# Row sums of a 16384 x 1024 matrix: VectorE takes the sixth whole block row by row as sums of halves

## The chip, the core and the metric

The kernel runs on one core of a Trainium2 chip. A time is the device time of one execution in microseconds (us). The time before is the median of three runs, 161.60 us, with runs from 161.56 to 161.78. A profile is one execution that the hardware profiler recorded; its times count from the first instruction of the recorded execution, and it is without the small stretch outside the program's first and last instruction.

## The reference

The input `x` is 32 x 512 x 1024 in fp32, 64 MiB. The output is the sum over the last axis, 32 x 512 numbers in fp32:

```python
def reference(x):
    return np.sum(x, axis=-1).astype(np.float32)
```

Every input number is read once and added once. The kernel is therefore a stream from device memory (HBM) to on-chip memory (SBUF), with sums that have to keep up with it.

## The kernel before

The 16384 rows are seen as eight blocks of 128 partitions x 16 rows x 1024 numbers. A block is 8 MiB, 64 KB in each partition. Block 7 is split: its first 7 rows are loaded first of all, and its other 9 rows last of all, in pieces of 6 rows, 2 rows, 536 numbers and 488 numbers of a row. Between them come the whole blocks 0 to 6 in order. So the stream is: 7 rows, blocks 0, 1, 2, 3, 4, 5, 6, then 6 rows, 2 rows and the two pieces of the last row.

`rows` (L177) loads a block, or a part of one, by one DMA from SyncE's queue (L180) and has it summed. There are two ways of summing on VectorE:

- `vec` (L140): one TENSOR_REDUCE over all the rows of the block, with one sum for each row.
- `halves` (L153): for each row one instruction that adds the first half of the row (512 numbers) to the second half, writes the 512 sums over the first half in place, and accumulates the sum of all. A second short instruction, DVE_READ_ACCUMULATOR2_ANT, writes the accumulated sum out. `rows` uses it where `pairs=True`.

ScalarE takes `n_act` of the rows (L166, an ACTIVATE with an accumulator and its readout; what it writes beside that goes unread to PSUM).

Blocks 0 to 5 and the first 7 rows are summed by `vec`, wholly on VectorE. Block 6 has 9 rows by `halves` and 7 rows on ScalarE. Of the last rows, the load of 6 has 4 rows by `halves` and 2 on ScalarE, the load of 2 has one of each, and the last row is summed in two pieces by two calls of `halves`, the second of which takes the first's sum in. "The sixth whole block" is block 5.

The order of the work on each engine is the order in which the kernel writes it (a manual schedule). The input tiles go round three buffers, which this text calls A, B and C: the first rows use A, then blocks 0 B, 1 C, 2 A, 3 B, 4 C, 5 A, 6 B, and the remaining rows of block 7 C. A load into a buffer waits until the sums of the buffer's earlier contents are done. The load of block 3 therefore waits for the sums of block 0, that of block 4 for block 1, that of block 5 for block 2, that of block 6 for block 3, and the last loads for block 4. No load follows into the buffers of blocks 5 and 6. SyncE issues loads strictly in order, so one that waits holds up those behind it. The load of block 1 is also held until the first rows are summed.

The sums of blocks 0 to 6 (56 KB) are stored by one DMA from ScalarE's queue, held until the load of two rows has landed; the sums of block 7 (8 KB) by one DMA of SyncE at the very end (L191 through L227).

## Time and profile before

| quantity | value | from |
|---|---|---|
| time, median of three runs | 161.60 us | the times |
| span of the profiled execution (its own time, first to last instruction) | 160.3 us | the page |
| difference of the two | 1.3 us | subtraction |
| VectorE busy | 120.6 us, 75% | the page |
| ScalarE busy | 11.9 us, 7% | the page |
| load queue (q1) | 67.12 MB, 97.7% of 16 DMA engines | the page |
| VectorE's sum of one whole block by one instruction | 17.22 us | groups by form |
| VectorE's sum of one row by halves | 0.689 us and a readout of 0.084 us | groups by form |

The page does not give a time of the profiled execution other than its span. A row of the groups names the line, the engine, the operation and the tile that it writes and reads, then the count, the busy time, the mean time of one in ns, and the idle time of the engine just before, with what ended it. The chain that ended last runs in time from the start to the end and names at each step what the next one waited for. In it the load steps overlap the sums before them, since a load is issued long before it is waited for.

The loads land, by the starts of the sums that wait for them, at 11.0 (7 rows), 30.3, 49.7, 69.1, 88.5, 108.0, 127.5 (block 5), 147.1 (block 6), 154.3 (6 rows), 156.8 (2 rows) and 158.1 us (the last piece).

### The profile page before, as it was taken

Reading aid. Unit: us, or ns where it says so; the run is one execution under the profiler, and the core shown is the slowest. Engines: PE = TensorE matmul, PEld = TensorE weight load, DVE = VectorE, ACT = ScalarE, POOL = GpSimd, SP = SyncE. Lnnn points to the kernel's source line nnn. Section 1 sums busy time; section 2 is a strip of 40 time slices with the busy share of each in tenths; the row PEclk is TensorE's granted clock in tenths of the full one; section 3 lists DMA queues with packets and bytes.
Section 4 is the critical chain, followed back from the end, with each engine's and each line's share of the span. In section 5 each row is a group of like instructions: output and inputs, shape, how many; then the busy total and the mean of one; then the engine's idle time right before and its main releaser. Section 6 shows DMA issues by size and latency. Waiting matters only on the chain.

```text
span 160.3 us, 132 instructions
## 1 busy us (share of the span) xinstructions
DVE 120.6 (75%) x40; ACT 11.9 (7%) x21; POOL 0.2 (0%) x4
## 2 busy tenths in 40 slices
DVE  0029600499986999679995999949999499994955
ACT  3000000000000000000000000000000000003993
POOL 0000000000000000000000000000000000000000
DMA  8999999899799699699699699796996996996994
GB/s 300 386 491 523 392 392 523 376 409 523 327 458 523 294 491 523 262 523 523 262 523 523 262 523 441 343 523 278 507 523 262 523 523 262 523 523 264 423 384 123
DMA packets 2784, 67.18 MB, mean 419 GB/s; under 512 B 1248, under 2 KB 1376, under 8 KB 1504
## 3 DMA queue, kind: packets, MB, share of 16 engines
q1 hardware_dynamic: 1872, 67.12, 97.7%
q10 hardware_dynamic: 912, 0.06, 0.4%
HBM read 67.11 MB, written 0.07 MB: 419 GB/s over the span
## 4 chain that ended last, share of the span: by engine, by line
DMA 71%; DVE 27%; SPq 1%; issue 0%; DVEq 0%
DMA t<-in_x_dram 71%; DVE sums L141 26%; SPq L180 0%; SPq L222 0%; DVE t L155 0%; DVEq L253 0%
## 5 line engine op out<-in xcount | busy, mean ns | idle before, releaser
L141 DVE TENSOR_REDUCE sums<-t 128x16 f32<-128x16384 f32 (+1 forms) x7 | 110.9, 15848 | 33.8 <-DMA t<-in_x_dram 33.8
L168 ACT ACTIVATE unread<-t 128x1024 f32<-128x1024 f32 x10 | 10.1, 1012 | 145.3 <-DMA t<-in_x_dram 145.3
L155 DVE CUSTOM_DVE_ANT_0 t<-t 128x512 f32<-128x512 f32 (+2 forms) x16 | 9.6, 656 | 4.1 <-DMA t<-in_x_dram 4.0
L168 ACT ACTIVATION_READ_ACCUMULATOR unread<-t 128x1 f32 x10 | 1.9, 187 | 0.0
L168 ACT ACT_TABLE_LOAD x1 | 1.3, 1283 | 0.8 <-PEq L242 0.8
L155 DVE DVE_READ_ACCUMULATOR2_ANT sums<- 128x1 f32 x15 | 1.3, 84 | 0.0
L242 POOL MEMSET const-bfloat16-1.0<- 128x1 bf16 x1 | 0.1, 101 | 0.0
L242 POOL MEMSET const-uint8-127<- 128x1 uint8 x1 | 0.1, 101 | 0.0
L242 POOL MEMSET const-float32-0.0<- 128x1 f32 x1 | 0.1, 98 | 0.2 <-issue 0.2
L242 POOL MEMSET const-float32-1.0<- 128x1 f32 x1 | 0.1, 98 | 0.0
L155 DVE DVE_READ_ACCUMULATOR2_ANT t<- 128x1 f32 x1 | 0.1, 83 | 0.0
L220 DVE MEMSET t<- 128x1 f32 x1 | 0.1, 59 | 0.0
## 6 DMA issues: line engine op xcount, KB each, us to landing
t<-in_x_dram SPq DMA_DIRECT2D x1, 3584.0 KB, 11.0
t<-in_x_dram SPq DMA_DIRECT2D x1, 3072.0 KB, 29.0
t<-in_x_dram SPq DMA_DIRECT2D x1, 1024.0 KB, 31.1
t<-in_x_dram SPq DMA_DIRECT2D x1, 268.0 KB, 31.4
t<-in_x_dram SPq DMA_DIRECT2D x1, 244.0 KB, 31.4
t<-in_x_dram SPq DMA_DIRECT2D x7, 41.1
out_dram<-sums ACTq DMA_DIRECT2D x1, 56.0 KB, 2.1
out_dram<-sums SPq DMA_DIRECT2D x1, 8.0 KB, 1.4
```

What stands on the lines that cost most here:

```text
L141: return nc.vector.tensor_reduce(out=dst, in_=src, axis=mybir.AxisListType.X, op=mybir.AluOpType.add)
L155: return nc.vector.tensor_tensor_reduce(out=src[:, :n], in0=src[:, :n], in1=src[:, n:], scale=1.0, scalar=0.0, op0=mybir.AluOpType.add, op ...
L168: nc.scalar.activation(out=unread[:, :n], in_=src, func=mybir.ActivationFunctionType.Copy, accum_out=dst,)
L220: nc.vector.memset(whole[:, width + 1 :], 0.0)
L242: nc = _bacc.Bacc("TRN2", target_bir_lowering=False, num_devices=1)
```

## The change

Block 5 is summed by `halves`, row by row, in place of one TENSOR_REDUCE over its 16 rows. Blocks 0 to 4 stay with `vec`, and block 6 stays as it was.

```diff
         for g in range(last):
             t = inpool.tile([P, BIG * dim + 4], fp32)
             if g < last - 1:
-                load = rows(t, 0, BIG, g * BIG, 0)
+                load = rows(t, 0, BIG, g * BIG, 0, pairs=g == last - 2)
             else:
                 rows(t, 0, BIG, g * BIG, 7, pairs=True)
```

On VectorE one TENSOR_REDUCE goes, and 16 sums of halves with 16 readouts come in its place, at the same place in the order; one wait on VectorE's own semaphore is added ahead of them, for the last reader of the buffer before (the sums of block 2), because `halves` writes into the tile. VectorE's whole program grows from 51 to 83 instructions, waits and barriers among them. The instructions of SyncE, ScalarE, GpSimd and TensorE are the same as before, in the same order.

## The prediction

> **What bounds the kernel now.** I began with the chain of work that ended last, because only work on it can move the end. Its second half, in the order of time (start, length, what), and after it three rows of the timeline (the same columns, with the idle time before in brackets):

> ```profile
> 66.94 41.09 DMA t<-in_x_dram
> 108.03 0.02 issue
> 108.05 17.23 DVE sums L141
> 125.28 0.02 issue
> 125.30 0.33 SPq L180
> ...
> 126.65 31.45 DMA t<-in_x_dram
> 158.09 0.04 issue
> 158.13 0.42 DVE t L155
> ```

> ```profile
> 108.05 17.22 DVE L141 TENSOR_REDUCE sums<-t 128x16 f32<-128x16384 f32 x1 [2.29 <-DMA t<-in_x_dram]
> ...
> 127.53 17.22 DVE L141 TENSOR_REDUCE sums<-t 128x16 f32<-128x16384 f32 x1 [2.27 <-DMA t<-in_x_dram]
> ...
> 147.06 0.69 DVE L155 CUSTOM_DVE_ANT_0 t<-t 128x512 f32<-128x512 f32 x1 [2.31 <-DMA t<-in_x_dram]
> ```

> The last sum of VectorE that the chain passes through is the one from 108.05 to 125.28, block 4: its end frees buffer C, SyncE issues the last four loads (125.30 to 127.1), and from then on the chain is the load stream up to 158.09, then 0.42 us of VectorE and the small store. Block 5's sum, the one that changes, runs from 127.53 and is not on it. Even the sum of block 4 is only on the chain by name: what it released was queued behind block 6's load, which landed at 147.06, more than 20 us later. So next I looked at the stream by stages, each from one landing to the next (columns: the stretch, its length, busy time of VectorE, ScalarE, GpSimd, then clock, DMA share, GB/s):

> ```profile
> 11.02:30.34 19.32, 7.62 (x1) 0.00 (x0) 0.00 (x0) 1.00 1.00 434
> 30.34:49.69 19.35, 17.22 (x2) 0.00 (x0) 0.00 (x0) 1.00 1.00 434
> 108.05:127.53 19.48, 17.22 (x1) 0.00 (x0) 0.00 (x0) 1.00 1.00 431
> 127.53:147.06 19.53, 17.22 (x1) 0.00 (x1) 0.00 (x0) 1.00 0.91 396
> 147.06:154.34 7.28, 5.60 (x18) 7.28 (x14) 0.00 (x0) 1.00 0.99 426
> 154.34:156.84 2.50, 2.50 (x8) 2.19 (x5) 0.00 (x0) 1.00 0.97 400
> ```

> A block takes 19.3 to 19.5 us to land and 17.22 us to sum. VectorE waits about 2.3 us in each stage for data. The DMA engines are full throughout. The kernel is bound by the load stream, with a short tail behind its last piece. (The GB/s of a stretch depends on where the records put its large packets, so the 396 of the fourth row is not read as a slow stage; the landing at 147.06, 19.53 us after the one before, is what counts.) Last, the groups by form, for durations:

> ```profile
> L141 DVE TENSOR_REDUCE sums<-t 128x16 f32<-128x16384 f32 x6 | 103.3, 17220 | 22.8 <-DMA t<-in_x_dram 22.8
> L155 DVE CUSTOM_DVE_ANT_0 t<-t 128x512 f32<-128x512 f32 x14 | 8.8, 689 | 4.0 <-DMA t<-in_x_dram 4.0
> L155 DVE DVE_READ_ACCUMULATOR2_ANT sums<- 128x1 f32 x15 | 1.3, 84 | 0.0
> ```

> **The change part by part.**

> *Removed:* one TENSOR_REDUCE of 17.22 us, from 127.53 to 144.75. *Added:* 16 sums of halves and 16 readouts. They overlap: in block 6 the nine row sums start at 147.06, 147.68, 148.29 and so on to 151.96 in the timeline, (151.96 - 147.06) / 8 = 0.6125 us apart. Sixteen rows take 15 x 0.6125 + 0.69 = 9.88 us, so block 5 should be summed at about 127.53 + 9.88 = 137.41, which is 144.75 - 137.41 = 7.3 us sooner.

> *Who waits for that end?* On VectorE, the sums of block 6, and they wait for a landing at 147.06: VectorE was idle 2.31 us before them and will be idle about 9.65. On SyncE, nothing: the last loads were issued from 125.30 to 127.1 on the end of block 4, before block 5's sum starts, and buffer A gets no later load. On ScalarE's queue, the store of the first seven blocks needs the sums, but it is also held until two rows land and was issued at 156.93, 12 us after block 5 was done. So the 7.3 us become idle time, worth 0 us. The cover is the landing of block 6. It would be gone only if block 5's sum ended after 147.06, that is if it took over 19.53 us, twice what I work out.

> *The added wait* on VectorE's own semaphore asks for the sums of block 2, done at 86.27 (69.05 + 17.22), 41 us before. The waits of this kind took 0.02 us each in the trace. It lies ahead of block 5's sums and behind block 4's, where VectorE waits 2.27 us for data anyway. Behind it stand only block 5's own sums. Cost 0 us, and 0.02 us if it came after the landing, which block 6's idle time would swallow.

> *A longer idle time ahead of block 6* is the one new state of VectorE. After 11.70 us of idle time it took up block 0 at 30.34 with the usual delay of 0.02 us and the usual 17.22 us, so I take 0.

> *What the new instructions do to the stream* is the only term that can move the end, since the stream of block 6 runs beside them. TENSOR_REDUCE reads SBUF and writes almost nothing; the halves read the same data and write half of it back (512 of 1024 numbers a row), in a shorter time. The trace of before has this beside loads only from 147.06 on. The 6-row load landed in 7.28 us with 5.60 us of VectorE beside it, almost all of it halves: 1.213 us a row. A row under TENSOR_REDUCE took 19.32 / 16 = 1.208 to 19.53 / 16 = 1.221 us. For six rows that is between 6 x (1.2133 - 1.2075) = +0.035 us and 6 x (1.2133 - 1.2206) = -0.04 us, by 5.6 us of halves; for 9.9 us of halves +0.06 to -0.08 us. A farther row gives the upper end: the 2-row load took 2.50 us, all of it under VectorE's halves, against 2 x 1.2075 = 2.415, so 0.085 us by 2.50 us, or +0.34 us by 9.9 us. [...] I take 0, from the 6-row load, which is the nearest in size, and keep +0.34 as the upper end.

> *Less of TENSOR_REDUCE beside the stream* could also be a gain. The stage with only 7.62 us of it took 19.32 us, stages with 17.22 us took 19.35 to 19.53: at most 0.21 us by 9.6 us, or 0.16 us for the 7.3 us that go. The stage of 19.35 with full VectorE work says that most of this is something else (0.03 by 9.6 us, or 0.02). I take 0 and keep -0.16 as the lower end.

> *Code.* 32 more instructions must be fetched. Inside the span the page's DMA queues are q1 and q10 alone, loads and stores; in the 12 us before the span there is another:

> ```profile
> DMA packets 13, 0.05 MB, mean 4 GB/s; under 512 B 7, under 2 KB 7, under 8 KB 7
> ## 3 DMA queue, kind: packets, MB, share of 16 engines
> q14 instruction: 13, 0.05, 1.4%
> ```

> Seven of the 13 packets are small, so six carry 0.05 MB, some 8 KB each, in 1.4% x 16 x 12 = 2.7 us of one engine: at most 0.45 us each. If 32 more instructions need one more such packet inside the span, one of the 16 DMA engines is late by up to 0.45 us, and by nothing at the end if it is not the last one. I take 0, since 83 instructions follow a program of 51 that needed none, and keep +0.45.

> *Sum:* 0 us on a span of 160.3 us; with the 1.3 us around it, the median of 161.6 stands as the forecast.

> [...]

> **The rivals.** What this kernel's measurement can tell from no change is about 0.2%, 0.32 us.

> 1. *Slower by a code fetch.* For it: the instruction queue exists, and VectorE's program is 63% longer. Against: none of its packets lies in the span before, with five engines' programs. Price: up to +0.45 us, 162.05, if the packet falls on a DMA engine that lands last. It passes the 0.32 us only in that case. If instead VectorE itself had to wait for code, it has 9.6 us of room up to 147.06 and 1.68 us more from 152.66 to 154.34.
> 2. *Slower by writes.* The in-place writes of halves hold up the stream's writes. For it: the 2-row load. Against: the 6-row load. Price: up to +0.34 us, 161.94, and it decides only at that upper end.
> 3. *Faster by less reading.* The shorter work of VectorE lets block 6 land sooner. For it: 19.32 against 19.53. Against: 19.35 with full work. Price -0.16 us, 161.44, which is still within 0.2%; it shows as faster only together with a favourable draw of runs.
> [...]

> **How the numbers follow.** The forecast (nothing moves, rival 4 included) has 0.72; the code fetch 0.11, the writes 0.10, the reading 0.07. Within 0.2% falls nearly all of the first (0.68, leaving 0.02 on each side for the two programs' runs not being alike), and of the others 0.03, 0.02 and 0.02: 0.75. Slower: 0.02 + 0.08 + 0.07 = 0.17, with 0.01 of the writes going the other way; faster: 0.02 + 0.05 + 0.01 = 0.08. The range goes down to rival 3 less the spread of runs, 161.44 - 0.12, about 161.3, and up to rivals 1 and 2, 162.0.

> **What would show it.** In the changed profile: 16 sums of halves from about 127.5 to 137.4, VectorE idle about 9.6 us before 147.1; landings at 127.5, 147.1, 154.3, 156.8 and 158.1 as before; q1 and q10 alone among the queues. Rival 1 would add an instruction queue to the span, rival 2 a landing of block 6 later than 19.53 us after block 5, rival 3 an earlier one. The prediction is wrong if block 6 lands more than 0.3 us off, or if VectorE begins block 6 later than its landing.

## The result and the profile after

The changed kernel takes 162.35 us (median, runs from 162.27 to 162.56) against 161.58 for the kernel before: ratio 1.0046, 95% interval 1.0033 to 1.0058. Run again beside the experiments it took 162.32, ratio 1.0035 (1.0023 to 1.0047). It is slower by 0.63 to 0.77 us by the medians. The forecast of no change was wrong, and the range ended at 162.0.

The profiled execution took 162.27 us with a span of 160.5. First the timeline of VectorE after (start, length, what, idle time before and what ended it; rows left out are marked by dots):

```profile
107.95 17.22 DVE L141 TENSOR_REDUCE sums<-t 128x16 f32<-128x16384 f32 x1 [2.13 <-DMA t<-in_x_dram]
...
127.30 0.69 DVE L155 CUSTOM_DVE_ANT_0 t<-t 128x512 f32<-128x512 f32 x1 [2.13 <-DMA t<-in_x_dram]
...
146.66 0.69 DVE L155 CUSTOM_DVE_ANT_0 t<-t 128x512 f32<-128x512 f32 x1 [9.47 <-DMA t<-in_x_dram]
...
154.60 0.69 DVE L155 CUSTOM_DVE_ANT_0 t<-t 128x512 f32<-128x512 f32 x1 [2.34 <-DMA t<-in_x_dram]
```

VectorE did what was forecast: block 5 from 127.30 to 137.19, then 9.47 us of idle time until block 6 lands. Nothing waited for it. The loss is further on. The stages after, each from one landing to the next (columns as in the prediction):

```profile
107.95:127.30 19.35, 17.22 (x1) 0.00 (x0) 0.00 (x0) 1.00 1.00 434
127.30:146.66 19.36, 9.89 (x33) 0.00 (x1) 0.00 (x0) 1.00 0.94 408
146.66:154.60 7.94, 5.60 (x19) 7.39 (x15) 0.00 (x0) 1.00 0.97 413
154.60:157.05 2.45, 2.45 (x7) 2.20 (x5) 0.00 (x0) 1.00 0.88 352
```

Block 6, whose load runs beside the new instructions, took 19.36 us, as the block before it did with its TENSOR_REDUCE. The load of six rows took 7.94 us, where it took 7.28 before: 0.66 us lost, in a stage in which VectorE and ScalarE do exactly what they did before. The queues of the page after have a line that the page before does not have:

```profile
q1 hardware_dynamic: 1872, 67.12, 97.3%
q10 hardware_dynamic: 912, 0.06, 0.4%
q14 instruction: 1, 0.01, 0.0%
```

and the half microsecond from 153.0 to 153.5 has it:

```profile
q1 hardware_dynamic: 34, 0.19, 98.6%
q14 instruction: 1, 0.01, 4.1%
```

One packet of code, 8 KB, lies at the time of the six-row load; 4.1% of 16 engines over 0.5 us is 0.33 us of one DMA engine. The chain ends as before, only later:

```profile
126.52 31.76 DMA t<-in_x_dram
158.27 0.02 issue
158.30 0.42 DVE t L155
```

The two profiled spans, 160.3 and 160.5, differ by only 0.2 us. Every later run has its span: 31 runs of the kernel before on one chip had a median of 159.8 (159.6 to 160.4), with 1.78 us around it, which is the time less the span. The execution that the prediction was read from was half a microsecond longer than most: its stages from 69 us on took 19.48 to 19.53 us, while those above took 19.35 and 19.36 (the execution above has two such longer stages early, of 19.49 and 19.47 us). Against 159.8, the changed kernel's median span of 160.5 has the whole loss, and the 1.78 us around it are the same.

### The profile page after: what moved, and what is told of

Read it like the earlier page. It is cut to its first block, busy times and chain, and to the rows that moved or that the text cites. A ratio compares the mean times of both kernels' runs of the same rounds, so it can differ in the third digit from the quotient of the medians.

```text
span 160.5 us, 164 instructions
## 1 busy us (share of the span) xinstructions
DVE 113.2 (71%) x71; ACT 12.0 (7%) x21; POOL 0.2 (0%) x4
## 4 chain that ended last, share of the span: by engine, by line
DMA 71%; DVE 26%; SPq 1%; issue 0%; DVEq 0%
DMA t<-in_x_dram 71%; DVE sums L141 26%; SPq L180 0%; SPq L222 0%; DVE t L155 0%; DVEq L253 0%
## 5 line engine op out<-in xcount | busy, mean ns | idle before, releaser
L141 DVE TENSOR_REDUCE sums<-t 128x16 f32<-128x16384 f32 (+1 forms) x6 | 93.7, 15620 | 31.4 <-DMA t<-in_x_dram 31.4
L155 DVE CUSTOM_DVE_ANT_0 t<-t 128x512 f32<-128x512 f32 (+2 forms) x32 | 19.4, 670 | 14.1 <-DMA t<-in_x_dram 14.1
L155 DVE DVE_READ_ACCUMULATOR2_ANT sums<- 128x1 f32 x31 | 2.5, 81 | 0.0
L155 DVE DVE_READ_ACCUMULATOR2_ANT t<- 128x1 f32 x1 | 0.1, 83 | 0.0
```

What stands on the lines that cost most here:

```text
L141: return nc.vector.tensor_reduce(out=dst, in_=src, axis=mybir.AxisListType.X, op=mybir.AluOpType.add)
L155: return nc.vector.tensor_tensor_reduce(out=src[:, :n], in0=src[:, :n], in1=src[:, n:], scale=1.0, scalar=0.0, op0=mybir.AluOpType.add, op ...
```

## The experiments

The code theory: VectorE's longer program makes it fetch one more block of code inside the span, and that packet puts back the DMA engine that it falls on, so that every load behind it lands late. A border, below, is in this theory the place in VectorE's program behind which another block of code is needed. The write theory: the in-place writes of the halves hold up the stream.

**The instructions without the writes.** The kernel before with 32 memsets, each of which writes one number that nobody reads:

```diff
         first = sums_of[-1]
+        spare = stpool.tile([P, 32], fp32)
+        for k in range(32):
+            nc.vector.memset(spare[:, k : k + 1], 0.0)
```

> The kernel before, with 32 one-number memsets on VectorE ahead of block 0's sum, where VectorE is idle for 11.7 us (18.65 to 30.34); block 5 is summed by one TENSOR_REDUCE as before. VectorE's program has 83 instructions, as many as the changed kernel. Code theory (one more code packet inside the span holds up one DMA engine): the queue q14 shows one packet inside the span at about 153 us, the 6-row load lands about 7.9 us after block 6 in place of 7.28, and the time is 0.3% to 0.6% above before (162.1 to 162.5). Write theory (the in-place writes of halves hold up the stream): no row by halves more than before, so no difference, 161.6.

Measured: 162.24 us, ratio 1.0036 (1.0024 to 1.0049), span 160.5. The loss is there in full, with block 5 summed as before. Its timeline, and its instruction queue between 153.0 and 153.5:

```profile
127.18 17.22 DVE L141 TENSOR_REDUCE sums<-t 128x16 f32<-128x16384 f32 x1 [2.13 <-DMA t<-in_x_dram]
146.62 0.69 DVE L155 CUSTOM_DVE_ANT_0 t<-t 128x512 f32<-128x512 f32 x1 [2.22 <-DMA t<-in_x_dram]
154.54 0.69 DVE L155 CUSTOM_DVE_ANT_0 t<-t 128x512 f32<-128x512 f32 x1 [2.33 <-DMA t<-in_x_dram]
```

```profile
q14 instruction: 1, 0.01, 3.9%
```

Six rows take 154.54 - 146.62 = 7.92 us, and the packet is where it was in the changed kernel.

**The writes without the instructions.** Block 5 by two instructions, the heart of the edit:

```diff
+                nc.vector.tensor_tensor(
+                    out=block[:, :, :half],
+                    in0=block[:, :, :half],
+                    in1=block[:, :, half:],
+                    op=mybir.AluOpType.add,
+                )
+                sums_of.append(vec(sums[:, j : j + nv], block[:, :, :half]))
```

> Block 5 by two instructions: one TENSOR_TENSOR that adds the halves of all 16 rows and writes them in place (the same bytes read and written in place as in the changed kernel), then one TENSOR_REDUCE over 16 x 512. The number of VectorE's instructions is as before, 51. VectorE should be at it for about 8.6 + 8.6 = 17.2 us. Code theory: no packet inside the span, 161.6. Write theory: the same loss as the changed kernel, 162.3, and block 6 lands late.

Measured: 161.64 us against 161.59, ratio 1.0007 (0.9998 to 1.0017), span 159.85 by the median, no packet of code in the profiled span. In the timeline the add with its in-place writes runs beside block 6's load:

```profile
127.73 8.69 DVE L183 TENSOR_TENSOR t<-t 128x8192 f32<-128x8192 f32 x1 [2.22 <-DMA t<-in_x_dram]
136.45 8.69 DVE L141 TENSOR_REDUCE sums<-t 128x16 f32<-128x8192 f32 x1
146.99 0.69 DVE L155 CUSTOM_DVE_ANT_0 t<-t 128x512 f32<-128x512 f32 x1 [1.85 <-DMA t<-in_x_dram]
```

Block 6 lands 19.26 us after block 5. The write theory falls: the same bytes written, in 8.69 us in place of 9.89, cost nothing that this measurement can tell.

**The packet at another place.** The changed kernel with 64 memsets, as in the first run, ahead of block 0's sum (147 instructions).

> The changed kernel, with 64 memsets in the same place. Code theory: VectorE crosses the border in its code early, at about 20 us, so the packet on q14 lies there and not at 153 us; the engine that is held up is late by the same amount for all that follows, so the time is again 0.3% to 0.6% above before, unless the engines' differences later swallow it. A second packet would show that the border recurs after fewer than 85 instructions. Write theory: as the changed kernel, 162.3, and the place of the packet is of no account.

Measured: 162.25 us, ratio 1.0035 (1.0023 to 1.0047), one packet, at 24.8 us. VectorE's timeline:

```profile
18.55 1.09 DVE L203 MEMSET spare<- 128x1 f32 x60
20.02 0.15 DVE L203 MEMSET spare<- 128x1 f32 x4 [0.38 <-issue]
31.01 17.22 DVE L141 TENSOR_REDUCE sums<-t 128x16 f32<-128x16384 f32 x1 [10.84 <-DMA t<-in_x_dram]
50.35 17.22 DVE L141 TENSOR_REDUCE sums<-t 128x16 f32<-128x16384 f32 x1 [2.12 <-DMA t<-in_x_dram]
```

Block 0 now lands at 31.0 in place of 30.3, and all that follows stays late by that. The same 0.65 us are paid at the other end of the stream. After 60 memsets VectorE stops for 0.38 us. With three instructions ahead of the block of the kernel and one sum, that is after its 64th instruction.

**How far the borders lie apart.** The kernel before with 192 memsets at that place.

> The kernel before with 192 memsets on VectorE in the idle time ahead of block 0's sum (some 15 ns each by the run with 32, 3 us of 11.7): 243 instructions. If code comes in packets of 8 KB that hold 128 instructions, VectorE crosses two borders, about its 62nd and its 190th instruction, both between 18 and 22 us: two packets on q14 inside the span. If each holds up one DMA engine by 0.65 us, the time is 0.65 above before when they fall on two engines (162.25) and 1.3 above when they fall on the same one (162.9). If packets are larger than 8 KB apart in the code, one packet alone and 162.25.

Measured: 163.35 us, ratio 1.0097 (1.0084 to 1.0109). VectorE's timeline:

```profile
18.62 1.09 DVE L203 MEMSET spare<- 128x1 f32 x60
20.10 3.63 DVE L203 MEMSET spare<- 128x1 f32 x128 [0.38 <-issue]
26.50 0.15 DVE L203 MEMSET spare<- 128x1 f32 x4 [2.78 <-issue]
31.94 17.22 DVE L141 TENSOR_REDUCE sums<-t 128x16 f32<-128x16384 f32 x1 [5.28 <-DMA t<-in_x_dram]
```

The borders stand after the 64th and the 192nd instruction, 128 apart, and there is a packet for each, at 24.7 and 30.4 us. Two packets cost 1.66 us, and block 0 lands at 31.9, with one of its 16 completions 1.55 us behind the next. If each of the 16 completions stands for one of the 16 DMA engines, two engines held up once each would leave two completions late; by that reading both packets fell on the same engine. The 0.38 us at the first border can't have been a wait for its packet, which came 4.6 us later, when VectorE was past the border; for which instructions the packet was, no run shows. At the second border VectorE stopped for 2.78 us and went on 1.5 us after the end of the first packet. That it had come there before its code would fit, but the profile doesn't show what it waited for.

**A border crossed when the loads are through.** The same edit with 16 memsets, 67 instructions.

> The kernel before with 16 such memsets: 67 instructions, so that VectorE reaches its 62nd at the very end of its work, when the last loads have landed or are about to. Code theory: the packet comes too late to hold up a load; what it costs depends on whether VectorE has to wait for it. If the fetch is ahead of need, 161.6 to 161.8; if the end of the program waits for it as in the run with three rows by halves, 0.4 us outside the last instruction or at the end of the span, 162.0; 162.25 would say that the place does not matter and the theory of the held-up engine is wrong.

Measured: 161.81 us against 161.69, ratio 1.0014 (1.0003 to 1.0024); the one packet lies at 160.0, behind the last load and just behind the span. The 6-row load lands 7.29 us after block 6. VectorE's 65th instruction begins 0.54 us after the 64th; in each of the other runs, the same two instructions of the program's end lie 0.11 apart. So the border is where the runs above put it, and of a stop of 0.42 us there at most 0.2 shows in the time. 16 more instructions cost about 0.1 us by the medians and 0.2 by the ratio, 32 cost 0.65.

**A border just behind the program.** Of block 5 only three rows by halves, 57 instructions (an excerpt; the call for block 5 sets `few`):

```diff
+            if few:
+                sums_of.append(vec(sums[:, j + 3 : j + nv], block[:, 3:nv, :]))
+                for q in range(3):
+                    sums_of.append(halves(sums[:, j + q : j + q + 1], block[:, q, :]))
```

> The kernel before, but of block 5 three rows are summed by halves and 13 by TENSOR_REDUCE: 57 instructions on VectorE in place of 51. Code theory: no packet inside the span (in the changed kernel it came when VectorE had come to about its 62nd instruction), and the time of before, 161.6 within 0.1. Write theory: 3/16 of the changed kernel's loss, about 0.15 us, 161.7.

Measured: 162.07 us, ratio 1.0025 (1.0012 to 1.0037), which neither theory had. The span is as before, 159.9 by the median, without a packet; the stretch around it is 2.18 us, where the kernel before has 1.78. So I tried the number of instructions alone, six memsets in place of the three rows:

> The kernel before with 6 memsets ahead of block 0's sum: 57 instructions on VectorE, as in the run with three rows by halves, and nothing else of that run. If the 0.4 us outside the span in that run come of the number of instructions, they come again: span 159.8, stretch around it 2.17 in place of 1.78, 162.0. If they came of the three rows by halves, 161.6.

Measured: 162.03 us, ratio 1.0025 (1.0013 to 1.0037), span 159.8, 2.20 us around it. It goes with the number. That the 0.4 us are a stop at the border, in code that runs behind the kernel's last instruction, fits the border after the 64th and the 0.42 us of the run with 16 memsets, but the profile shows nothing there, so it stays an argument.

**Whose code.** GpSimd with 100 memsets, VectorE as before (the line inside the loop):

```diff
+            nc.gpsimd.memset(spare[:, k : k + 1], 0.0)
```

> The kernel before with 100 one-number memsets on GpSimd, which has no other work, from the start on; VectorE's program is as before, 51 instructions. Code theory: any engine's code packet holds up the stream, so q14 shows one packet in the first 15 us or so and the time is 162.25. If only VectorE's code matters (it stands ahead of the sums), 161.6.

Measured: 161.84 us against 161.69, ratio 1.0004 (0.9995 to 1.0014), with an 8 KB packet at 6.1 us. Either the early time or the engine made it cheap. Two pairs of runs tell these apart. VectorE early, in the kernel before and in the changed one:

```diff
+        for k in range(66):
+            nc.vector.memset(spare[:, k : k + 1], 0.0)
         j = last * BIG
```

> The kernel before with 66 memsets on VectorE ahead of its first sum: VectorE comes to its 64th instruction at about 2 us and the packet lies in the first 10 us, when only the load of 7 rows is in flight. If the price of a packet goes by when it comes (GpSimd's at 6.1 us put one engine back by about 0.36 us, VectorE's at 24.8 and 153 by 0.65 to 0.7), the time is 0.1 to 0.3 above before; if it goes by whose code it is, 0.65 above, 162.3.

> The changed kernel with the same 66 memsets ahead of the first sum: 149 instructions, one border crossed at about 2 us and none later. If the price goes by when the packet comes, this kernel is faster than the changed kernel although it has 66 instructions more: about 161.9. If it goes by whose code it is, 162.3 as the changed kernel.

Measured: 162.24 us, ratio 1.0035 (1.0023 to 1.0047), and 162.23, ratio 1.0038 (1.0025 to 1.0050), with one packet each, at 7.2 and 6.1 us. The loss is the same 0.6 us when VectorE's packet comes early. It is also the same for 149 instructions as for 83, and with or without the change: what counts is one border crossed. And GpSimd late, its memsets held behind one memset of VectorE at 18.6 us:

```diff
+        nc.vector.memset(spare[:, :1], 0.0)
+        for k in range(100):
+            nc.gpsimd.memset(spare[:, k : k + 1], 0.0)
```

> The 100 memsets on GpSimd again, but held until VectorE has summed the first 7 rows (18.7 us; one memset more on VectorE): the packet falls at about 25 us, as VectorE's did in the run with 64 memsets more. If the price goes by when the packet comes, 0.65 us above before, 162.3; if GpSimd's code costs the stream less than VectorE's, 161.8.

Measured: 161.86 us against 161.61, ratio 1.0009 (1.0000 to 1.0018). Its packet lies at 24.7 us, as VectorE's did in the run with 64 memsets. The timeline, to hold against 31.01 there and 30.34 in the kernel before:

```profile
18.76 3.36 POOL L204 MEMSET spare<- 128x1 f32 x100 [18.33 <-DVE spare L202]
30.58 17.22 DVE L141 TENSOR_REDUCE sums<-t 128x16 f32<-128x16384 f32 x1 [11.90 <-DMA t<-in_x_dram]
```

At the same moment of the stream, GpSimd's packet puts the landing back by about 0.2 us and VectorE's by 0.65. It goes by whose code it is, and the trace's records of single DMA packets show where the difference lies. They don't name the DMA engine, so the load packet that begins as a code packet ends (1 ns after it in the changed kernel) is taken for the next one on the same engine. It is longer than others of its size:

| run | whose code | code packet: start, length (us) | load packet behind it (us) | usual for its size | longer by |
|---|---|---|---|---|---|
| changed kernel | VectorE | 153.08, 0.33 | 8 KB, 0.95 | 0.31 | 0.64 |
| changed kernel again | VectorE | 152.50, 0.31 | 24 KB, 1.48 | 0.91 | 0.57 |
| before, 32 memsets | VectorE | 153.13, 0.31 | 8 KB, 0.87 | 0.31 | 0.57 |
| changed, 64 memsets | VectorE | 24.82, 0.31 | 64 KB, 2.97 | 2.42 | 0.55 |
| before, 192 memsets | VectorE | 24.74, 0.31 | 64 KB, 2.96 | 2.42 | 0.54 |
| the same, second packet | VectorE | 30.42, 0.33 | 64 KB, 3.07 | 2.42 | 0.65 |
| before, 66 early | VectorE | 7.20, 0.31 | 28 KB, 1.60 | 1.06 | 0.54 |
| changed, 66 early | VectorE | 6.10, 0.31 | 28 KB, 1.59 | 1.06 | 0.53 |
| 100 on GpSimd | GpSimd | 6.09, 0.31 | 28 KB, 1.28 | 1.06 | 0.22 |
| 100 on GpSimd, late | GpSimd | 24.75, 0.31 | 64 KB, 2.63 | 2.42 | 0.22 |

By that reading a packet of VectorE's code takes 0.84 to 0.98 us from its DMA engine, its own time and what the load packet behind it takes longer; one of GpSimd's takes 0.53. (The 0.22 of the early run on GpSimd says little, since some 28 KB packets before 5 us are as long without code ahead of them, up to 1.86 us in the kernel before; the late run has no such neighbours.) Not all of it reaches the landing, because the 16 completions of a load don't come together: without a packet the 16 completions of one of the larger loads spread over 0.3 to 0.6 us, and behind one packet of VectorE one of them trails the next by 0.56 to 0.80 us for the rest of the stream, behind one of GpSimd by 0.2 to 0.4. Of the 0.43 us between the landings at 31.01 and 30.58, 0.33 are in the packet behind the code. Why that packet takes longer was not found, nor whether the difference comes of the engine whose code it is or of the DMA engine that moves it.

## Why the prediction was wrong

*What bounds the kernel, and what the change does on VectorE:* right. Block 5 is summed in 9.89 us (9.88 forecast), VectorE is idle 9.47 us ahead of block 6 (9.65), no wait appeared on another engine, and the 7.3 us saved are worth nothing.

*The writes beside the stream:* right at 0, and now measured in two ways: block 6 landed in 19.36 us beside them, and the run with the writes alone is at 1.0007. So nothing supports the upper end of 0.34, from the 2-row load; what its 0.085 us come from, no run tests.

*Less of TENSOR_REDUCE:* right at 0. Stages of 19.35 us appear under 17.22 us of it and 19.36 under none.

*Code:* this is the step that failed, "I take 0, since 83 instructions follow a program of 51 that needed none". It inferred from a program that stops short of a border that a longer one stops short too. The border after the 64th instruction lay between the two; in the runs the borders are 128 instructions apart and the packets 8 KB, a size that the prediction had from the packets ahead of the span, and still it counted 0. The rival named the mechanism, its queue and its sign ("Rival 1 would add an instruction queue to the span"), and had 0.11. Its price was mis-sized as well: "at most 0.45 us each" was a mean (the six packets took 0.31 to 0.55 us), and it took the packet's own time for the whole delay. A packet of 0.33 us put the last landing back by 0.65 to 0.7, since the load packet behind it took 0.53 to 0.65 us longer too. So even with the rival as the forecast, 162.05 would have been 0.3 us short.

*The rest of the sum:* "the 1.3 us around it" set one execution's span beside the median of other executions. By the later runs the stretch is 1.78 us. This did not move the forecast, which was made against the median, but it hid that the profiled execution was longer than most.

*Rival 4*, which the 0.72 takes in, has VectorE no quicker with the change. No run shows that: the 16 rows of block 5 start 0.613 us apart, as the nine of block 6 did, and the block takes 9.89 us where one TENSOR_REDUCE took 17.22.

## What to carry to other kernels

In this kernel, whose loads take 97.7% of the 16 DMA engines' span, the number of VectorE's instructions was itself a cost, in steps: replacing one long instruction by 32 short ones cost 0.65 us through one packet of code, although VectorE had 9.47 us of idle time behind them. In another kernel, look for the instruction queue in the profile, inside the span and before it, and where a change adds instructions to an engine, ask how near the program stands to its next border (here after VectorE's 64th and 192nd instruction); measure that with idle memsets, which took 15 to 29 ns each here (32 in 0.49 us, 61 in 1.75 us). And before a span is set beside a median, see whether both are of the same execution.
